# Bias rows of a decoder layer: one broadcast store to DRAM becomes a small store and a copy inside DRAM

## The chip, the cores and the metric

The kernel runs on one core of a Trainium2 chip. The metric is the device time of one execution in microseconds (us), taken as the median of several runs. The profile is one more execution, recorded instruction by instruction. The engines are named as the profile names them: PE is TensorE's matmul, PEld its weight load, DVE is VectorE, ACT is ScalarE, POOL is GpSimd and SP is SyncE, which here only issues transfers. POOL and SP each have a transfer queue of their own (q0 "software" and q1 "hardware" in the profile); both run on the same 16 DMA engines.

## The reference, cut to what matters

One decoder layer for 512 tokens of width 2048. An input projection gives a gated convolution and the queries, keys and values of three groups of eight attention heads. Each group attends with its own dilation (1, 4 and 16 tokens), and to its scores a bias is added that depends on the distance between query and key alone:

```python
steps = qi + BLK - ki
in_window = (steps >= 0) & (steps <= n_steps)
bucket = _t5_bucket(np.clip(steps, 0, None) * dilation)
bias = jnp.take(bias_table, jnp.asarray(bucket), axis=0)
...
scores = scores + bias[:, None]
scores = jnp.where(valid, scores, jnp.finfo(jnp.float32).min)
```

The three groups are mixed by their softmax denominators, an output projection and a LayerNorm follow, then a gated MLP with a width-3 convolution and a second LayerNorm. Everything is float32.

## The kernel before, in words

**The projection.** The 96 column tiles of the input projection are worked off as 48 pairs: twelve for the convolution (u, c, b four times), then 36 for q, k and v. `run_pairs` computes one pair as seven Strassen-like products; each is 24 matmuls in `product` (lines 326 to 328), so a pair has 168. The weights of a pair come as two loads of 1 MB (`load_next`, line 156) into a ring of three `raw` buffers, issued on SP; a load waits until the ring's oldest buffer has been read. `Op.front` and `Op.back` form differences of weights where the product needs them (line 181), round them to `whi` (line 191, ACT) and take the rest as `wlo` (line 194, DVE). There are four `whi` and four `wlo` buffers, so ACT and DVE can be up to four products ahead of PE.

**The outputs of a pair.** About two products after the last one that a half needs, `combine` adds PSUM and a snapshot into a tile `o` of 128 x 1024 (line 572 for q, k, v of group 0, line 581 for the others; the profile names it by these lines). `done1` then stores it: to `yc_d` (line 606) for the convolution, to `qkv_d` (line 611) for q, k and v, both on POOL's queue. The tiles `o` come from a pool of three buffers (`otile1`); a new one waits until the last reader of that buffer is done, which for a store is its landing.

**The bias rows.** After the last convolution pair `bias_setup` runs for the three groups, one every seven products. It takes one of the three `o` buffers as scratch, loads a one-hot matrix (line 555) and a mask (line 556) into it on SP's queue, and five products later `finish` multiplies the bias table with the one-hot matrix (line 560), adds the mask (line 561) and leaves eight rows, one for each head, in partitions 0 to 7: 383 numbers for group 0, 255 for groups 1 and 2. Line 563, on POOL's queue, stores each row 128 times into `seq_d`. Between two calls of `bias_setup` the pairs take `o` buffers from the same pool: the buffer of group 0's rows is next used by the second q, k, v pair, and the scratch of group 2 is the buffer of the first such pair, free when that pair's `qkv_d` store has landed.

**The reader.** `seq_d` is read in the attention, by `toep` in `a_load` (lines 634 to 637): with a step of 383 elements from one copy to the next, each of the 128 partitions reads its row shifted by one, which gives the bias of a block of queries and keys.

The order of the work is that of the program: each engine runs its instructions in the order written, and `later` and `tick` place the deferred parts by a count of products.

Of the kernel before, what the change touches and what calls it, by code (L numbers as in the profile page):

```python
# [12 lines left out]
F32 = mybir.dt.float32  # L13
# [5 lines left out]
P = 128  # L19
# [3 lines left out]
NH = 8  # L23
# [72 lines left out]
def layer_kernel(ctx: ExitStack, tc: tile.TileContext, xT, x, w_in, w_out, w_up, w_down, cw, fw, lnp, lnc, table,  # L96
                 onehot, mask, out):
    nc = tc.nc
# [6 lines left out]
    dram = ctx.enter_context(tc.tile_pool(name="dram", bufs=1, space=bass.MemoryType.DRAM))  # L105
# [15 lines left out]
    def get_bank():  # L121
        i = free_banks.pop(0)
        return i, bank(i)
# [4 lines left out]
    n_d = dram.tile([4, P, D], F32, name="n_d")  # L128
    act_d = dram.tile([P, FT, S], F32, name="act_d")
    seq_d = dram.tile([3, NH, P, 384], F32, name="seq_d")  # L130
    stA_d = dram.tile([NH, S, 2], F32, name="stA_d")
    stB_d = dram.tile([NH, S, 2], F32, name="stB_d")

# [158 lines left out]
    def later(n, fn):  # L292
        pending.append([n, fn])
# [205 lines left out]
    i, b = get_bank()  # L499
# [45 lines left out]
    def otile1():  # L545
        return tp.tile([P, 4, 256], F32, tag="o", name=nm("o"), bufs=3)

    def bias_setup(g=0):
        if g == 0:
            held["tb"] = tp.tile([32, 3 * NH], F32, name="tb")  # L550
            nc.gpsimd.dma_start(held["tb"], table)
        a, b = [0, LA, LA + LB, LTOT][g:g + 2]
        v = otile1().rearrange("p a b -> p (a b)")
        oh, mk = v[:32, 0:b - a], v[:NH, 512:512 + b - a]
        nc.sync.dma_start(oh, onehot[:, a:b])
        nc.sync.dma_start(mk, mask[:, a:b])

        def finish():
            i, ps = get_bank()
            mm(ps[:NH, :b - a], held["tb"][:, g * NH:(g + 1) * NH], oh, start=True, stop=True)  # L560
            nc.vector.tensor_add(mk, ps[:NH, :b - a], mk)
            free_banks.append(i)
            nc.gpsimd.dma_start(seq_d[g, :, :, :b - a], mk[:, None].to_broadcast([NH, P, b - a]))
            if g < 2:
                later(2, lambda: bias_setup(g + 1))

        later(5, finish)
# [505 lines left out]
    for q in range(NQ - 1):  # L1073
        for c in range(4):
# [3 lines left out]
            if c == 1 and q + 2 < NQ:  # L1078
                if q == 0:
                    load_gb(0)  # L1080
                b = (q + 2) % 3
# [118 lines left out]
```

## Time and profile before

| | us |
|---|---|
| median of 3 runs | 2673.99 (2672.46 to 2676.1) |
| the profiled execution's own time | 2674.91 |
| its span, first to last instruction | 2673.0 |
| PE busy in the span | 2624.3 (98%) |
| DVE, ACT, POOL busy | 2015.5, 1159.3, 124.4 |

The mean granted clock of TensorE is 0.992 of full speed. A busy PE is not a PE at full speed: at half the clock its instructions take longer and count as busy all the same, so the number of matmuls in a stretch says more than its busy time. The projection's pairs for q, k and v begin at about 265 us and end at about 1020 us.

### The profile page before, as it was taken

What the parts mean: (1) busy time and instruction counts of PE and PEld (TensorE: products, weight loads), DVE (VectorE), ACT (ScalarE), POOL (GpSimd) and SP (SyncE); (2) the same over time, 40 slices, a digit from 0 to 9 for tenths busy, and PEclk for the clock granted to TensorE, in tenths of its full rate; (3) what the DMA queues carried; (4) which work ended last, traced back from release to release, by engine and by line L of the source; (5) the groups of instructions that cost most, each with busy time, mean ns of one, the idle gap of its engine ahead of it and who ended that gap; (6) DMA issues with size and microseconds to landing.
All of it is one profiled execution on the core that took longest, in us unless ns stands there. A gap on an engine that the chain in (4) does not pass through costs nothing.

```text
span 2673.0 us, 45078 instructions
## 1 busy us (share of the span) xinstructions
PE 2624.3 (98%) x19114; PEld 2497.2 (93%) x19114; DVE 2015.5 (75%) x2293; ACT 1159.3 (43%) x1617; POOL 124.4 (5%) x214
## 2 busy tenths in 40 slices
PE   9999889999999999999999999999999999999998
PEld 8999789999999998888999999999999998888886
DVE  7987557777777777666899888888888875675557
ACT  5444334444444444434655555555555553222220
POOL 0000000000000002221000000000000000000000
PEclk9999989999999999999999999999999999999999
DMA  7433653333333338644543333333333354434331
GB/s 240 166 103 128 111 138 125 134 129 132 135 123 139 134 119 312 221 160 160 182 144 131 117 123 111 123 123 108 126 119 111 127 181 156 149 142 148 120 126 63
DMA packets 70905, 376.69 MB, mean 141 GB/s; under 512 B 10608, under 2 KB 14440, under 8 KB 36016
## 3 DMA queue, kind: packets, MB, share of 16 engines
q1 hardware_dynamic: 51680, 311.47, 34.0%
q0 software_dynamic: 19024, 62.34, 7.3%
q8 instruction: 150, 2.46, 0.4%
q14 instruction: 51, 0.42, 0.1%
HBM read 324.95 MB, written 48.81 MB: 140 GB/s over the span
## 4 chain that ended last, share of the span: by engine, by line
PE 88%; DVE 5%; DMA 4%; ACT 1%; issue 1%; SPq 0%; DVEq 0%; POOL 0%; ACTq 0%
PE bk L326 21%; PE bk L328 21%; PE bk L327 21%; PE bk L423 8%; PE bk L421 8%; PE bk L422 8%; DMA raw<-in_w_in_dram 2%; DMA seq_d<-o 2%; DVE wlo L194 1%; DVE tt L181 1%; PE bk L744 1%; PE bk L690 1%; PE bk L674 0%; ACT whi L191 0%; PE bk L736 0%
## 5 line engine op out<-in xcount | busy, mean ns | idle before, releaser
L191 ACT ACTIVATE whi<-raw 128x1024 fp32r<-128x1024 f32 x394 | 416.0, 1058 | 631.9 <-PE bk L423 219.0
L194 DVE TENSOR_TENSOR wlo<-raw,whi 128x1024 fp32r<-128x1024 f32 x394 | 480.7, 1223 | 216.0 <-ACT whi L191 215.9
L194 DVE TENSOR_TENSOR wlo<-tt,whi 128x1024 fp32r<-128x1024 f32 x360 | 440.5, 1224 | 210.1 <-ACT whi L191 209.5
L191 ACT ACTIVATE whi<-tt 128x1024 fp32r<-128x1024 f32 x360 | 379.6, 1054 | 220.1 <-PE bk L327 122.7
L326 PE MATMUL bk<-S,whi 128*128 128x256 f32 x1440 | 409.2, 284 | 12.4 <-ACT sm L374 11.5
L327 PE MATMUL bk<-S,whi 128*128 128x256 f32 x1440 | 408.4, 284 | 0.0
L328 PE MATMUL bk<-S,wlo 128*128 128x256 f32 x1440 | 408.4, 284 | 0.0
L326 PEld LDWEIGHTS bk<-S,whi 128*128 128x128 f32 x1440 | 277.5, 193 | 13.6 <-ACT sm L374 11.9
L327 PEld LDWEIGHTS bk<-S,whi 128*128 128x128 f32 x1440 | 277.5, 193 | 0.0
L328 PEld LDWEIGHTS bk<-S,wlo 128*128 128x128 f32 x1440 | 277.4, 193 | 0.0
L181 DVE TENSOR_TENSOR tt<-raw,tt 128x1024 f32<-128x1024 f32 x180 | 219.1, 1217 | 36.6 <-DMA raw<-in_w_in_dram 36.6
L326 PE MATMUL bk<-A22h,whi 128*128 128x256 f32 x752 | 212.8, 283 | 0.0
L327 PE MATMUL bk<-A22l,whi 128*128 128x256 f32 x752 | 212.8, 283 | 0.0
L328 PE MATMUL bk<-S3h,wlo 128*128 128x256 f32 x752 | 212.8, 283 | 0.0
L327 PE MATMUL bk<-S3l,whi 128*128 128x256 f32 x752 | 212.8, 283 | 0.0
L326 PE MATMUL bk<-S3h,whi 128*128 128x256 f32 x752 | 212.8, 283 | 0.0
L328 PE MATMUL bk<-A22h,wlo 128*128 128x256 f32 x752 | 212.8, 283 | 0.0
L328 PE MATMUL bk<-S1h,wlo 128*128 128x256 f32 x720 | 205.1, 285 | 6.2 <-DVE wlo L194 6.2
L326 PE MATMUL bk<-A1h,whi 128*128 128x256 f32 x720 | 205.2, 285 | 0.6 <-ACT S L932 0.6
L326 PE MATMUL bk<-S1h,whi 128*128 128x256 f32 x720 | 204.7, 284 | 0.0
L327 PE MATMUL bk<-S1l,whi 128*128 128x256 f32 x720 | 204.7, 284 | 0.0
L328 PE MATMUL bk<-A1h,wlo 128*128 128x256 f32 x720 | 204.4, 284 | 0.0
(225 smaller groups left out, 6435.4 us busy)
## 6 DMA issues: line engine op xcount, KB each, us to landing
raw<-in_w_in_dram SPq DMA_DIRECT2D x97, 1024.0 KB, 4.9
raw<-in_w_up_dram SPq DMA_DIRECT2D x89, 1024.0 KB, 5.3
raw<-in_w_down_dram SPq DMA_DIRECT2D x44, 1024.0 KB, 4.9
qkv_d<-o POOLq DMA_DIRECT2D x36, 512.0 KB, 4.3
raw<-in_w_out_dram SPq DMA_DIRECT2D x16, 1024.0 KB, 6.8
act_d<-z POOLq DMA_DIRECT2D x44, 256.0 KB, 5.2
qk<-qkv_d SPq DMA_DIRECT2D x7, 1536.0 KB, 10.3
ar<-act_d SPq DMA_DIRECT2D x9, 1024.0 KB, 7.0
```

The source lines that it names most:

```text
L181: nc.vector.tensor_sub(self.src, v[0], prev)
L191: nc.scalar.activation(self.hi, self.src, AF.Copy)
L194: nc.vector.tensor_sub(self.lo, self.src, self.hi.bitcast(F32))
L326: mm(ps, op.hi[:, w], xh[:, k], start=first and k == 0, stop=False, skip_group_check=True)
L327: mm(ps, op.hi[:, w], xl[:, k], start=False, stop=False, skip_group_check=True)
L328: mm(ps, op.lo[:, w], xh[:, k], start=False, stop=last and k == 7, skip_group_check=True)
L421: mm(banks[n], yh[:, tt], op.hi[:, w], start=first and i == 0, stop=False)
L422: mm(banks[n], yh[:, tt], op.lo[:, w], start=False, stop=False)
L423: mm(banks[n], yl[:, tt], op.hi[:, w], start=False, stop=last and i == 1)
L690: mm(ps[:, o:o + P], qk[:, 2 + 2 * g, rs], qk[:, 3 + 2 * g, rs], start=True, stop=True)
L744: nc.tensor.transpose(ps[:, i * P:(i + 1) * P], src[:, n, s:s + P], ident)
```

## The change

The eight rows go once into a new DRAM tensor `seq1_d`. A second transfer, from DRAM to DRAM, makes the 128 copies in `seq_d`; its outer loop runs over the 128 copies and the heads lie inside it. Both are on POOL's queue, and the second reads what the first has written. The contents of `seq_d` and its readers are as before.

```diff
     seq_d = dram.tile([3, NH, P, 384], F32, name="seq_d")
+    seq1_d = dram.tile([3, NH, 384], F32, name="seq1_d")
...
             nc.vector.tensor_add(mk, ps[:NH, :b - a], mk)
             free_banks.append(i)
-            nc.gpsimd.dma_start(seq_d[g, :, :, :b - a], mk[:, None].to_broadcast([NH, P, b - a]))
+            nc.gpsimd.dma_start(seq1_d[g, :, :b - a], mk)
+            nc.gpsimd.dma_start(seq_d[g, :, :, :b - a].rearrange("h p n -> p h n"),
+                                seq1_d[g, None, :, :b - a].to_broadcast([P, NH, b - a]))
             if g < 2:
                 later(2, lambda: bias_setup(g + 1))
```

## Rows read from the trace of the kernel before

**Rows 1.** The page: PE's busy time, and the chain's shares by line.
```profile
PE 2624.3 (98%) x19114; PEld 2497.2 (93%) x19114; DVE 2015.5 (75%) x2293; ACT 1159.3 (43%) x1617; POOL 124.4 (5%) x214
...
PE bk L326 21%; PE bk L328 21%; PE bk L327 21%; PE bk L423 8%; PE bk L421 8%; PE bk L422 8%; DMA raw<-in_w_in_dram 2%; DMA seq_d<-o 2%; DVE wlo L194 1%; DVE tt L181 1%; PE bk L744 1%; PE bk L690 1%; PE bk L674 0%; ACT whi L191 0%; PE bk L736 0%
```
**Rows 2.** The chain in order of time, 278 to 380 us: start, length, what.
```profile
278.90 40.53 DMA seq_d<-o
```
**Rows 3.** Stretches: length, busy time and count per engine, PEclk, DMA share, GB/s.
```profile
280.00:400.00 120.00, 96.30 (x731) 94.08 (x730) 63.57 (x64) 36.30 (x47) 5.86 (x8) 0.89 0.60 126
400.00:520.00 120.00, 120.00 (x1002) 120.00 (x1002) 88.43 (x86) 51.00 (x66) 4.29 (x6) 1.00 0.37 130
...
300.00:310.00 10.00, 8.69 (x73) 8.49 (x72) 3.81 (x4) 2.27 (x3) 1.10 (x1) 1.00 0.60 124
```
**Rows 4.** Timeline of DVE, four of its instructions between 262 and 320 us.
```profile
262.22 0.68 DVE L572 TENSOR_TENSOR o<-bk,sm 128x512 f32<-128x512 f32 x1
...
283.30 0.68 DVE L572 TENSOR_TENSOR o<-bk,sm 128x512 f32<-128x512 f32 x1
...
303.98 1.23 DVE L181 TENSOR_TENSOR tt<-raw,tt 128x1024 f32<-128x1024 f32 x1 [9.07 <-DMA raw<-in_w_in_dram]
...
319.46 0.69 DVE L572 TENSOR_TENSOR o<-bk,sn 128x512 f32<-128x512 f32 x1 [11.67 <-DMA seq_d<-o]
```
**Rows 5.** Waits, 255 to 420 us: who <- whom: us, times, longest.
```profile
PE bk L326 <- ACT sm L374: 10.6, 1, 10.6
...
PE bk L560 <- DMA o<-in_onehot_dram: 6.9, 1, 6.9
...
PE bk L328 <- DVE wlo L194: 6.2, 2, 4.9
```
**Rows 6.** DMA issues, 279 to 308 us: times, KB each, median us to landing.
```profile
raw<-in_w_in_dram SPq DMA_DIRECT2D x2, 1024.0 KB, 21.3
...
qkv_d<-o POOLq DMA_DIRECT2D x1, 512.0 KB, 36.7
```
**Rows 7.** DMA issues of the whole span (columns of Rows 6).
```profile
raw<-in_w_in_dram SPq DMA_DIRECT2D x97, 1024.0 KB, 4.9
...
qkv_d<-o POOLq DMA_DIRECT2D x36, 512.0 KB, 4.3
...
gb<-in_lnp_dram SPq DMA_DIRECT2D x4, 1024.0 KB, 9.1
...
seq_d<-o POOLq DMA_DIRECT2D x1, 1532.0 KB, 40.5
...
stA_d<-st POOLq DMA_DIRECT2D x8, 4.0 KB, 6.3
...
tb<-in_table_dram POOLq DMA_DIRECT2D x1, 3.0 KB, 2.8
```
**Rows 8.** Timeline of SP's queue: two weight loads, 281.54 and 11 us later.
```profile
281.54 11.20 SPq L156 DMA_DIRECT2D raw<-in_w_in_dram  x2
```
**Rows 9.** The waits of SP's queue, 255 to 425 us.
```profile
SPq L555 <- DMA qkv_d<-o: 28.2, 1, 28.2
```
**Rows 10.** Timeline of POOL: start, length, instruction, [idle before <-releaser].
```profile
278.90 1.10 POOL L563 DMA_DIRECT2D seq_d<-o  x1 [13.40 <-DVE o L561]
284.28 0.74 POOL L611 DMA_DIRECT2D qkv_d<-o  x1 [4.28 <-DVE o L572]
...
398.94 0.72 POOL L611 DMA_DIRECT2D qkv_d<-o  x1 [17.16 <-DVE o L581]
419.09 0.71 POOL L611 DMA_DIRECT2D qkv_d<-o  x1 [19.44 <-DVE o L581]
```
**Rows 11.** A stretch with one `seq_d` store alone (columns of Rows 3).
```profile
290.00:293.00 3.00, 3.00 (x27) 3.00 (x27) 1.86 (x2) 1.52 (x3) 0.00 (x0) 1.00 0.48 49
```
**Rows 12.** DMA queue, 308 to 318 us: packets, MB, share of 16 engines.
```profile
q0 software_dynamic: 132, 0.58, 91.8%
```
**Rows 13.** Users of `seq_d`: ns min/median/max, first and last start in us.
```profile
L634 POOL DMA_DIRECT2D ba<-seq_d x1: 553/553/553, 1008.5 to 1008.5; - x1
```

## The prediction, as it was put on record before the result was known

> **What bounds the kernel now.** I read the page first. PE is busy for 98% of the span and its matmul lines make up nearly all of the chain, so only what stops PE, or slows it, can move the time; but one transfer stands in that chain too, the store of the bias rows, with 2% [rows 1]. The chain in order of time shows where: group 0's store, issued at 278.90 us, is 40.53 us of it in one piece [rows 2]. So I took the stretch around it and compared it with the next one of the same length: 731 matmuls in 280 to 400 us against 1002 in 400 to 520 us, with a mean granted clock of 0.89 against 1.00 [rows 3]. PE idles there, and for part of the time after it idled it runs at the lower of its two levels. The question is how much of that is the three stores' doing, and whether the copies that replace them do the same again.
>
> The waits of the stretch name three ways in which a store of 40 us reaches PE. First, the scratch: `o` stays taken until the store lands, and DVE's combine waits 11.67 us for it [rows 4]; PE then stands 10.6 us behind the snapshot [rows 5]. Second, the weights: two loads of 1 MB took 21.3 us to land [rows 6] where the median of 97 is 4.9 [rows 7]; DVE waited 9.07 us for the one issued at 281.54 [rows 4, 8], and later PE stood 6.2 us for weights of this kind [rows 5]. Third, the queue: the first pair's `qkv_d` store, issued behind the bias store, took 36.7 us to land [rows 6]; SP waited 28.2 us for it before it could load group 2's one-hot matrix [rows 9], and PE 6.9 us for that matrix [rows 5].
>
> **What the change can give back.** The q, k, v stores are a clock of the pairs. From 398.94 to 419.09 one pair takes 20.15 us [rows 10]. From 284.28 to 419.09 there are five pairs (the stores at 323, 353 and 381 us are not shown): 134.81 us less 5 x 20.15 leaves 34.06. Not all of it is a stall: the bias matmuls themselves cost PE something, and group 0's price, before any bias store was in flight, is the distance from the combine at 262.22 to that at 283.30, 21.08 less 20.15 = 0.93 us [rows 4]. Groups 1 and 2 keep that: 1.86. So 32.2 us are stall. By matmuls it is 120 x (1002 - 731) / 1002 = 32.5 us, less 1.86 = 30.6 [rows 3]. I take the middle, 31.4 us, and both as ends. Idle time and the lower clock behind it are both in these numbers.
>
> **What it adds, step by step.**
>
> The small store, 12 KB from eight partitions: no row has this shape. The nearest are a 3 KB load on the same queue, 2.8 us to landing, and 4 KB of statistics stored in pieces of 8 bytes, 6.3 us [rows 7]. It is a store, but with rows of 1.5 KB; I take 4 us. It frees the scratch at about 283 instead of 319.4. The second pair's combine came for it at 319.46 - 11.67 = 307.8, and without the weights' 9 us before that would come at about 299. The first of the three ways is gone, for any price between the two ends.
>
> The wait on POOL: the copy reads what the store wrote, so POOL stands until that lands, 278.90 + 4 = 282.9. The copy's issue takes the 1.10 us of the present one [rows 10], up to 284.0. Queued behind is only the `qkv_d` store of 284.28 [rows 10], so this costs nothing; at 6.3 us it would be issued 2 us late, and nobody needs it for another 8.
>
> The copy itself, 1532 KB for group 0. No row moves DRAM to DRAM. From below: a 1 MB load lands in 4.9 us, so 1.5 MB hardly in less than 7.3. From above: the present store of the same rows, 40.5 us [rows 7]. Which end is nearer depends on why the store is slow. Alone, it keeps 0.48 of the DMA engines busy and moves 49 GB/s [rows 11]; when two overlap, the engines are 91.8% busy and the same queue moves 0.58 MB in 10 us, 58 GB/s [rows 12]. Twice the engines gave hardly more rate, so the limit is shared: either the eight source partitions or the rows written. The q, k, v stores write DRAM at well over that, 512 KB in 4.3 us or 119 GB/s with all their fixed cost [rows 7], but out of 128 partitions and in longer rows; the few partitions are the larger difference, and I take the source as the cause. The copy's source is instead one stretch of 12 KB in DRAM read 128 times. That has a near row: `gb` reads one DRAM row 128 times, 1 MB in 9.1 us to landing, four of them, issued in pairs by line 1059 [rows 7]. I take 9.1 x 1532 / 1024 = 13.6 us, and 9.1 for groups 1 and 2 (1020 KB).
>
> What waits for the copies. The readers of `seq_d` come at 1008.5 [rows 13], 700 us later: nothing. The first pair's `qkv_d` store lies behind the copy on the queue: 282.9 + 13.6, and about 4 for itself, is 300.5. SP waits for it from about 292.7 (320.95 less 28.2), and behind that wait on SP is the next weight load, due at 281.54 + 20.15 = 301.7: nothing lost. The one-hot matrix is then there by about 306, and its matmul is due two pairs after group 0's, which the store of 278.90 followed, so not before 317.
>
> The weight load of 281.54 runs beside the copy. If it got no engine at all until the copy had landed, it would land at 282.9 + 13.6 + 4.9 = 301.4 against the 294.9 at which DVE asked for it (303.98 less 9.07): 6.5 us late. That is covered: DVE's 9.07 us of waiting cost PE only 10 - 8.69 = 1.3 us in 300 to 310 [rows 3], because ACT and DVE work ahead of PE by some 7.8 us. Groups 1 and 2 meet the same pattern 20 and 40 us later with shorter copies. So a copy costs nothing up to about 13.6 - 6.5 + 7.8 = 14.9 us, and I cost all three at nothing; the cover is the 7.8 us of finished weights.
>
> **The sum** against the profiled execution: 2674.91 - 31.4 = 2643.5 us. That execution is 0.9 above the median of the runs shown, 2673.99; from there it is 2642.6. I say 2643. About 0.2%, 5.3 us, is what a measurement of this kernel can tell from no change.
>
> [...] One bias store alone holds only 0.48 of the engines, and two 0.92 [rows 11, 12]: a weight load had half of the engines free. [...]
>
> For how long weights wait beside such a transfer, the row is 21.3 us to landing instead of 4.9 [rows 6, 7]. [...]
>
> **The rivals.** Let D be the time of group 0's copy, and two thirds of it for the others, and let weights get nothing while a copy runs. PE then idles D - 14.9 for group 0, and 0.67 D - 14.9 for each of the others, where these are above nothing. In the present stretch PE's idle time, 120 - 96.3 = 23.7 us [rows 3], went with a loss of 31.4, so each us idle costs 1.3.
>
> *All engines are held for a middling time.* The copy takes about 22 us, because it reads and writes the same memory and its rows are 1.5 KB: 22 - 14.9 = 7.1 us idle, times 1.3, is 9 us given back: 2652. For it: no row shows such a copy. Against it: `gb` moves more than three times as fast. Chance 0.10.
>
> *The written rows are the limit, and it becomes slower.* If the 128 x 8 rows of 1532 bytes were what held the store to 49 GB/s, the copy would be no faster, and it would hold all engines. Then 40.5 - 14.9 = 25.6 and 2 x 12.2 are 50.0 us idle, 65 with the clock, against 31.4 now: 2708. It decides from D = 29 on, where 2.34 D - 44.7 reaches 23.7. For it: the two causes leave the same rate. Against it: the first pair's store of 512 KB and other DRAM writes share these engines and land in a few us elsewhere. Chance 0.08.
>
> *It does not do what it says.* The copy, D between 27 and 31, is as long as the stall that it replaces, or the scratch stays taken because the small store lands late in a busy queue: within 5 us of 2674. Chance 0.06.
>
> **How the numbers follow.** The forecast has 0.76, and its own spread is 2639 to 2647 (30.6 to 32.2, the runs' own 2 us, a few us for one stall that I miss). The first rival has 0.10 at 2652. The range 2639 to 2657 takes in both and leaves out the two others, 0.14, and some of the tails. Faster by over 0.2%: 0.76 + 0.10 = 0.86; within: 0.06; slower: 0.08.
>
> **What would show it.** In the profile after: no wait of DVE for `seq_d` or `seq1_d`, no wait of SP for `qkv_d` at line 555, about 990 matmuls in 280 to 400 us with a clock of 1.00, five pairs in some 102.7 us from the first `qkv_d` store, and copies that land in 7 to 14 us. A copy over 20 us, or weight loads that still land in over 15, would show the first rival; copies of 30 us and more the second. The forecast is wrong if PE still idles in this stretch for more than a few us.

## The result, and the profile after

The changed kernel takes 2643.47 us (median of four runs, 2643.22 to 2643.77), the kernel before 2674.87 beside it. The ratio is 0.9884, with a 95% interval of 0.9867 to 0.9901: 31.4 us, 1.2%, faster.

The page of the changed kernel, its first part and its chain by line:

```profile
PE 2616.5 (99%) x19114; PEld 2490.2 (94%) x19114; DVE 2016.7 (76%) x2293; ACT 1159.4 (44%) x1617; POOL 125.8 (5%) x217
...
PE bk L327 22%; PE bk L328 22%; PE bk L329 22%; PE bk L424 8%; PE bk L422 8%; PE bk L423 8%; DVE wlo L195 1%; DVE tt L182 1%; PE bk L747 1%; DMA raw<-in_w_in_dram 1%; PE bk L693 0%; ACT whi L192 0%; PE bk L677 0%; DMA ycr<-yc_d 0%; PE bk L739 0%
```

Lines are shifted by one to three against before. `seq_d` is gone from the chain [rows 1]. PE was busy longer before (2624.3 us) with the same 19114 matmuls: some of them had run at the lower clock (0.89 granted in 280 to 400 us [rows 3]). What that does to a busy PE two stretches of the kernel before show: 11 matmuls from 324 to 326 us at a clock of 0.50, 19 from 328 to 330 us at 1.00, and PE counts as busy for all of both.

The stretches that answer to [rows 3] (length, busy time and count per engine, PEclk, DMA share, GB/s):

```profile
280.00:400.00 120.00, 120.00 (x994) 118.87 (x993) 87.19 (x85) 49.99 (x65) 8.16 (x11) 1.00 0.49 163
400.00:520.00 120.00, 120.00 (x1002) 120.00 (x1001) 86.96 (x85) 51.05 (x66) 4.30 (x6) 1.00 0.38 132
300.00:310.00 10.00, 10.00 (x85) 10.00 (x85) 7.45 (x8) 3.72 (x5) 1.64 (x2) 1.00 0.68 201
```

994 matmuls stand where 731 stood, at full clock, and PE does not idle. POOL's timeline, the new pair of transfers and the stores that mark the pairs (start, length, instruction, [idle before <-releaser]):

```profile
278.72 0.52 POOL L564 DMA_DIRECT2D seq_d<-o  x1 [13.38 <-DVE o L562]
280.69 0.94 POOL L565 DMA_DIRECT2D seq_d<-seq_d  x1 [1.45 <-DMA seq_d<-o]
284.10 0.74 POOL L614 DMA_DIRECT2D qkv_d<-o  x1 [2.48 <-DVE o L575]
...
387.23 0.72 POOL L614 DMA_DIRECT2D qkv_d<-o  x1 [19.45 <-DVE o L584]
```

From 284.10 to 387.23 there are five pairs, 103.13 us; before they took 134.81 [rows 10]. That difference, 31.7 us, is the whole change: from the sixth such store to the end it is 2673.0 - 419.1 = 2253.9 us before and 2641.7 - 387.2 = 2254.5 after. POOL waits 1.45 us for the small store to land, then issues the copy, and is idle again before the next `qkv_d` store is ready: nothing waits for it.

The transfers issued from 279 to 308 us (times, KB each, median us to landing), which answer to [rows 6]:

```profile
raw<-in_w_in_dram SPq DMA_DIRECT2D x3, 1024.0 KB, 5.0
seq_d<-seq_d POOLq DMA_DIRECT2D x1, 1532.0 KB, 11.1
qkv_d<-o POOLq DMA_DIRECT2D x2, 512.0 KB, 8.2
seq_d<-seq_d POOLq DMA_DIRECT2D x1, 1020.0 KB, 9.5
o<-in_onehot_dram SPq DMA_DIRECT2D x1, 31.9 KB, 4.3
seq_d<-o POOLq DMA_DIRECT2D x1, 12.0 KB, 1.7
```

The copy lands in 11.1 us instead of 40.5, the weights in 5.0 (median of three) instead of 21.3 (of two), the `qkv_d` stores in 8.2 (of two) instead of 36.7. Of SP's waits for a transfer this one is left (255 to 425 us: who <- whom: us, times, longest), where 28.2 stood [rows 9]:

```profile
SPq L556 <- DMA qkv_d<-o: 0.4, 1, 0.4
```

### The profile page after: what moved, and what is told of

It is laid out like the page before. It is cut to its first block, busy times and chain, and to the rows that moved or that the text cites. A ratio compares the mean times of both kernels' runs of the same rounds, so it can differ in the third digit from the quotient of the medians.

```text
span 2641.7 us, 45080 instructions
## 1 busy us (share of the span) xinstructions
PE 2616.5 (99%) x19114; PEld 2490.2 (94%) x19114; DVE 2016.7 (76%) x2293; ACT 1159.4 (44%) x1617; POOL 125.8 (5%) x217
## 4 chain that ended last, share of the span: by engine, by line
PE 91%; DVE 5%; DMA 1%; ACT 1%; issue 1%; SPq 0%; POOL 0%; DVEq 0%; ACTq 0%
PE bk L327 22%; PE bk L328 22%; PE bk L329 22%; PE bk L424 8%; PE bk L422 8%; PE bk L423 8%; DVE wlo L195 1%; DVE tt L182 1%; PE bk L747 1%; DMA raw<-in_w_in_dram 1%; PE bk L693 0%; ACT whi L192 0%; PE bk L677 0%; DMA ycr<-yc_d 0%; PE bk L739 0%
## 5 line engine op out<-in xcount | busy, mean ns | idle before, releaser
L328 PE MATMUL bk<-A1l,whi 128*128 128x256 f32 x720 | 204.4, 284 | 0.0
```

Of the source, the lines that this page charges most:

```text
L328: mm(ps, op.hi[:, w], xl[:, k], start=False, stop=False, skip_group_check=True)
```

## The experiments

The times of the experiments are medians of four to ten runs, with the kernel before timed on the same chip (2673.8 to 2674.0 us; 2674.87 for the changed kernel). "Store" is the time to landing of group 0's bias store or copy, "weights" that of the first weight load issued beside it, "matmuls" the count in 280 to 400 us; these three are from one profiled execution each. The ratios are against the kernel before; no interval was taken between two edits.

| run | edit | us | ratio, 95% interval | store | weights | matmuls |
|---|---|---|---|---|---|---|
| before | | 2674 | | 40.5 | 22.3 | 731 |
| after | the change | 2643.5 | 0.9867 to 0.9901 | 11.1 | 8.6 | 994 |
| e4_fullrows | whole rows written | 2673.3 | 0.9984 to 1.0003 | 39.6 | 22.3 | 741 |
| e6_from128 | store from 128 partitions | 2643.6 | 0.9873 to 0.9902 | 7.1 | 9.8 | 993 |
| e9_spread4 | from 8, four apart | 2642.7 | 0.9868 to 0.9899 | 13.4 | 9.8 | 995 |
| e10_spread16 | from 8, sixteen apart | 2643.1 | 0.9869 to 0.9904 | 23.0 | 14.5 | 989 |
| e5_heads_outer | copy, heads outside | 2647.0 | 0.9881 to 0.9914 | 13.5 | 5.3 | 995 |
| e1_scratch | own scratch | 2670.6 | 0.9978 to 0.9997 | 41.8 | 23.0 | 768 |
| e2_actq | store on ACT's queue | 2667.6 | 0.9966 to 0.9985 | not recorded | 21.1 | 791 |
| e3_both | both | 2661.6 | 0.9936 to 0.9966 | not recorded | 21.4 | 839 |
| e7_copy2 | two copies | 2648.0 | 0.9889 to 0.9919 | 19.2 (both) | 9.6 | 995 |
| e8_copy4 | four copies | 2644.0 | 0.9880 to 0.9909 | 32.7 (all) | 9.5 | 931 |
| e11_held | four copies, scratch held | 2662.1 | 0.9939 to 0.9970 | 32.4 (all) | 9.5 | 846 |

### Why the store was slow

**The rows written (e4_fullrows).** Edit, on the kernel before (the mask gets one column more, and the sum leaves that column as loaded):

```diff
-            nc.gpsimd.dma_start(seq_d[g, :, :, :b - a], mk[:, None].to_broadcast([NH, P, b - a]))
+            nc.gpsimd.dma_start(seq_d[g, :, :, :b - a + 1], mk[:, None].to_broadcast([NH, P, b - a + 1]))
```

> The kernel before, storing rows of 384 and 256 numbers (1536 and 1024 bytes) instead of 383 and 255, so that each row written is whole and follows the last without a gap; the extra number is a mask value that no reader uses. Theory, the eight source partitions set the store's rate: still about 40 and 24 to 34 us to land, about 49 GB/s alone, 2675 us within 4. Rival, the written rows with their gaps set it: under 20 us to land and under 2655.

Nothing changed: 39.6 us to landing, and 2673.3 us. The gaps between the rows do not set the rate; the rows themselves are tested next.

**The source partitions (e6_from128, e9_spread4, e10_spread16).** The three are one store out of SBUF, as before. Their table has each head's column repeated, so that the matmul leaves the row in several partitions; what is stored differs. For e9_spread4 (the mask row is loaded into all partitions):

```diff
-            held["tb"] = tp.tile([32, 3 * NH], F32, name="tb")
-            nc.gpsimd.dma_start(held["tb"], table)
+            tb = tp.tile([32, 3 * NH], F32, name="tb")
+            nc.gpsimd.dma_start(tb, table)
+            held["tb"] = tp.tile([32, 3 * 32], F32, name="tbr")
+            nc.vector.tensor_copy(held["tb"].rearrange("p (h c) -> p h c", c=4),
+                                  tb[:, :, None].to_broadcast([32, 3 * NH, 4]))
...
-            nc.gpsimd.dma_start(seq_d[g, :, :, :b - a], mk[:, None].to_broadcast([NH, P, b - a]))
+            nc.gpsimd.dma_start(seq_d[g, :, :, :b - a], mk[::4, None].to_broadcast([NH, P, b - a]))
```

e10_spread16 has 16 in place of 4, and e6_from128 stores all 128 partitions eight times each:

```diff
+            nc.gpsimd.dma_start(seq_d[g].rearrange("h (c r) n -> (h c) r n", r=8)[:, :, :b - a],
+                                mk[:, None].to_broadcast([P, 8, b - a]))
```

> One broadcast store from SBUF as in the kernel before, on POOL's queue, but out of 128 partitions: the bias table's columns are repeated 16 times, so that the matmul leaves each head's row in 16 partitions, and each partition is stored eight times. The rows written are the same; there is no copy in DRAM and no wait on POOL. Theory, the eight source partitions set the rate: lands in 5 to 12 us, 2643 us within 4. Rival, the written rows set it: about 40 us and 2670 or over.

The question to the two spread stores is whether the number of the source partitions held the store or their place; that the place would count was my estimate, and no run had shown it then.

> The store of the kernel before, in the same order and with the same outer loop of eight heads, but the eight source rows lie in partitions 0, 4, 8 ... 28 instead of 0 to 7 (the bias table's columns are repeated four times, and every fourth row is stored). [...] Rival, each partition gives only so much whichever it is: still about 40 us, 2674. [...]

> The same with the eight source rows in partitions 0, 16, 32 ... 112, repeated sixteen times. [...] Rival, any spreading is as good, or the wider the better: 8 to 12 us. [...]

All three are as fast as the changed kernel within 1 us, with no copy in DRAM. The row to compare is POOL's DMA queue in the same three us, 281 to 284 (packets, MB, share of 16 engines). The kernel before:

```profile
q0 software_dynamic: 316, 0.16, 56.3%
```

e9_spread4:

```profile
q0 software_dynamic: 470, 0.62, 57.4%
```

The rows written, their order and, within two per cent, the busy share of the engines are the same, and four times as many bytes go out. In the store only the eight source partitions differ. So neither the written rows nor the number of engines held the store; reading from neighbouring partitions did. The landing times are 40.5 us for 0 to 7, 23.0 for steps of sixteen, 13.4 for steps of four and 7.1 for all 128. "Farther apart" would have put the step of sixteen ahead of the step of four, so it is not the distance alone that counts; what else does, no run shows. I had taken the eight partitions as the cause; eight of them elsewhere gave 13.4 us, so it is not their number alone but where they lie.

**The outer loop (e5_heads_outer).** Edit, on the changed kernel:

```diff
-            nc.gpsimd.dma_start(seq_d[g, :, :, :b - a].rearrange("h p n -> p h n"),
-                                seq1_d[g, None, :, :b - a].to_broadcast([P, NH, b - a]))
+            nc.gpsimd.dma_start(seq_d[g, :, :, :b - a],
+                                seq1_d[g, :, None, :b - a].to_broadcast([NH, P, b - a]))
```

> The changed kernel, with the heads instead of the copies as the outer loop of the DRAM to DRAM copy: the same rows are read and written, in another order. Theory, the source partitions made the store slow: the copy stays fast, landing in 8 to 16 us with half of the engines or more, and the time is that of the changed kernel, 2643 us within 4. Rival, an outer loop of eight (half of the engines) made it slow: 30 us and more to land, and 2655 or over.

The copy lands in 13.5 us, and alone it keeps half of the engines busy (a stretch of e5_heads_outer, columns of [rows 3]):

```profile
290.00:293.00 3.00, 3.00 (x28) 3.00 (x27) 1.34 (x2) 1.33 (x2) 0.00 (x0) 1.00 0.52 202
```

Group 0's weight load lands in 5.3 us beside it instead of 8.6, but group 2's in 8.5 instead of 9.6, so what the free engines are worth to a load is not settled. PE gains nothing from them: 995 matmuls, full clock. The 3.5 us above the changed kernel lie elsewhere. The profiled execution is 4.7 us longer; 1.3 of them have passed when the first `qkv_d` store is issued, and 3.6 lie between the last `qkv_d` store and the last `v` load of the attention, 157.8 us against 154.2. At the start of that stage the load of `yc_d` takes 12.96 us instead of 10.93. The pairs between the first and the last `qkv_d` store take as long as in the changed kernel, 706.0 us.

### How a slow store reached PE

**Own scratch (e1_scratch).** Edit, on the kernel before:

```diff
         oh, mk = v[:32, 0:b - a], v[:NH, 512:512 + b - a]
+        if g < 2:
+            mk = tp.tile([P, 384], F32, tag="bs", name=nm("bs"), bufs=2)[:NH, :b - a]
```

> The kernel before, but the sums of groups 0 and 1 lie in buffers of their own, so that the slow store no longer holds a buffer that the pairs need (group 2 stays as it was). Theory, three ways that stand in a row: the 11.7 us wait of DVE for the scratch goes, but the first pair's qkv_d store still lands at about 321 us behind the bias store, SP still stands for it, and the weights come late instead: about 2668 us, between 2661 and 2675. Rival, the held scratch is the whole stall: 2643 to 2650 us. The bias stores themselves still take 24 to 41 us to land.

2670.6 us: 3.4 of 31 us come back. The waits of e1_scratch, 255 to 420 us (who <- whom: us, times, longest):

```profile
DVE tt L181 <- DMA raw<-in_w_in_dram: 44.2, 3, 22.5
...
PE bk L328 <- DVE wlo L194: 21.6, 3, 14.8
```

DVE's wait for the scratch is gone, and so is SP's for the `qkv_d` store, because group 2's one-hot matrix went into a buffer that group 1's matmul had freed. In their place DVE waits 44.2 us for weights where it had waited 36.6, and PE 21.6 for what DVE makes of them where it had waited 6.2 [rows 5]. The kernel before, in the same view:

```profile
DVE tt L181 <- DMA raw<-in_w_in_dram: 36.6, 3, 15.5
```

So e1_scratch came out as the third way alone, and that alone costs 2670.6 - 2643.5 = 27 us. It is the third way in a stronger form: SP, no longer held up, issues two loads at 310 to 317 us, beside two bias stores, and they take 31.7 and 29.5 us; the kernel before issued them at 322 us and later, and the first took 23.3.

**Another queue (e2_actq, e3_both).** Edit, alone and on top of e1_scratch:

```diff
-            nc.gpsimd.dma_start(seq_d[g, :, :, :b - a], mk[:, None].to_broadcast([NH, P, b - a]))
+            nc.scalar.dma_start(seq_d[g, :, :, :b - a], mk[:, None].to_broadcast([NH, P, b - a]))
```

> The kernel before, with the bias stores issued on ACT's queue instead of POOL's; the scratch is held as before. Theory: the first pair's qkv_d store no longer lies behind the bias store and lands in under 10 us, SP does not stand for it at the one-hot load, and the 6.9 us wait of PE for the one-hot matrix goes; the wait of DVE for the scratch (about 11 us) and late weights stay: about 2661 us, between 2655 and 2670. Rival, the queue does not matter because the weights are what is late: over 2670.

> Both edits at once: bias stores on ACT's queue, the sums of groups 0 and 1 in buffers of their own. Only the third way is left, weights that share engines with a slow store. Theory: weight loads beside a bias store still take 12 to 22 us to land, 4 to 9 us too late for DVE, which the finished weights mostly cover: 2645 to 2652 us. Rival, the slow weights are a stall of their own: over 2655.

e2_actq gives back 6.4 us, in the range, but not quite as expected: the `qkv_d` store lands in 19.8 us instead of 36.7, not in under 10, and SP still stands 11.3 us for it. The bias store was still busy beside it, on ACT's queue, with 44.4% of the engines (283 to 285 us); that this is the reason is likely, and no run shows it. e3_both missed, 2661.6 instead of 2645 to 2652. Its waits show the rival's picture, slow weights as a stall of their own:

```profile
DVE tt L181 <- DMA raw<-in_w_in_dram: 35.2, 3, 16.5
...
PE bk L328 <- DVE wlo L194: 13.8, 3, 9.6
```

It is no clean test of the third way, since SP stood 12.2 us for a `qkv_d` store and 8.6 us for a bias store before it issued weights.

**The first two ways without the third (e11_held).** Edit, on e8_copy4 below: behind the four copies a store of the scratch, which therefore stays taken until they are through.

```diff
+            nc.gpsimd.dma_start(last_d[g, :, :b - a], mk)
```

> The kernel with four copies, and behind them on POOL's queue one more small store out of the scratch, so that the scratch stays taken until the copies are through, some 35 us, as with the store of the kernel before; there is no slow packet for the weights to stand behind. The first two ways without the third. Theory now, each way alone is enough for a stall: DVE waits for the scratch by 10 to 16 us in group 0 and again later, 2658 to 2675 us. Rival, only the slow weights made the stall and the scratch costs little alone: under 2652.

In e11_held a packet of POOL's queue kept an engine busy for 0.19 us (44.4% of 16 engines for 13 us, 478 packets, from 279 to 292 us), in the kernel before for 0.67 (48.9% of 16 for 5 us, 58 packets, from 288 to 293 us). That a weight load stands behind such a packet no run shows.

2662.1 us, 18.6 above the changed kernel. The waits of e11_held name the scratch (DVE's combine is L581 here) and hardly the weights:

```profile
DVE o L581 <- DMA last_d<-o: 27.5, 2, 14.7
...
PE bk L329 <- ACT sm L377: 14.3, 2, 8.1
...
DVE tt L184 <- DMA raw<-in_w_in_dram: 0.2, 1, 0.2
```

Late weights alone cost 27 us, held scratch with the blocked queue 19, and all together 31. The ways overlap: while PE stands for one, the others run out. That is why undoing one or two of them gave little. The blocked queue nearly alone is e8_copy4 below: 0.5 us in the median of four runs, 7 in one of them.

### What a long copy costs

**More copies (e7_copy2, e8_copy4).** Edit, on the changed kernel, with j up to 1 or 3:

```diff
+            for j in range(3):
+                nc.gpsimd.dma_start(more_d[j, g, :, :, :b - a].rearrange("h p n -> p h n"),
+                                    seq1_d[g, None, :, :b - a].to_broadcast([P, NH, b - a]))
```

> The changed kernel with a second copy, to another DRAM tensor, behind each copy. Theory, a copy costs nothing up to about 14.9 us: the last of group 0's copies lands 15 to 18 us after the first was issued, the qkv_d store behind it by about 300 us, and the time stays within 4 us of 2643. Rival, each us of copy costs something: 2650 or over.

> The changed kernel with three more copies behind each copy, to other DRAM tensors. Theory: group 0's copies together last about 26 us, the others about 19; beyond 14.9 us each us of copy idles PE and costs 1.3: 11 x 1.3 for group 0, 4 x 1.3 for each of the others, 2667 us, between 2655 and 2680; SP stands for the qkv_d store at the one-hot load again. Rival, weights and copies take turns and the cover holds: 2643 to 2650.

e7_copy2 lies 4.5 us above the changed kernel, just outside "within 4". Its stretch has no stall, 995 matmuls at full clock, and as in e5_heads_outer the attention is longer, 158.0 us. e8_copy4 contradicts the expectation: copies that last 32.7 us together take 2644.0 us in the median, as the rival said, and not 2667. Its four runs are 2643.3, 2643.8, 2644.2 and 2650.7, and the last is the profiled one. There the first weight load beside the copies lands early (issues from 279 to 292 us: times, KB each, median us to landing):

```profile
more_d<-seq_d POOLq DMA_DIRECT2D x3, 1532.0 KB, 27.6
seq_d<-seq_d POOLq DMA_DIRECT2D x1, 1532.0 KB, 14.0
raw<-in_w_in_dram SPq DMA_DIRECT2D x1, 1024.0 KB, 9.5
qkv_d<-o POOLq DMA_DIRECT2D x1, 512.0 KB, 30.4
```

The `qkv_d` store takes 30.4 us, nearly as long as beside the slow store, and SP stands 22.0 us for it. The weight load takes 9.5 us, not 22.3, and the second one, issued 11 us later, 13.4 instead of 20.2. PE works through all of this at full clock until 320 us. What the profiled execution loses comes after it: because SP stood, its next weight load goes out at 316.85 us instead of 302.27 in the changed kernel, and takes 13.0 us beside group 1's copies. The waits of e8_copy4, 255 to 420 us:

```profile
DVE tt L183 <- DMA raw<-in_w_in_dram: 21.8, 3, 13.9
...
PE bk L330 <- DVE wlo L196: 6.1, 1, 6.1
```

So in this execution the long copies reached PE by the queue, the second way. Why the three other runs escape stays open, since none of them has a trace.

In the view of the issues from 279 to 292 us, e10_spread16:

```profile
seq_d<-o POOLq DMA_DIRECT2D x1, 1532.0 KB, 23.0
raw<-in_w_in_dram SPq DMA_DIRECT2D x1, 1024.0 KB, 14.5
qkv_d<-o POOLq DMA_DIRECT2D x1, 512.0 KB, 19.7
```

Its second load takes 10.8 us. The two first loads thus take 22.3 and 20.2 us beside the slow store of 40.5, 14.5 and 10.8 beside a store of 23.0, and 9.5 and 13.4 beside 32.7 us of copies that, with the loads, keep 0.97 of the engines busy from 283 to 288 us. How long the other transfer lasts does not set this; its pace is the likelier cause, but the last two cases lie too close to show that. How the slow store delays a load can be seen in part. From 288 to 293 us of the kernel before, with one load out since 281.54, the queues have this one line:

```profile
q0 software_dynamic: 58, 0.26, 48.9%
```

That is POOL's queue. SP's moved no packet, though the engines were idle for half of the time.

## Why the prediction was right, and where a step was not

The forecast was 2643 us, and 2643.47 was measured.

**The size of the stall** was right: 31.4 us forecast, from 32.2 by the stores and 30.6 by the matmuls; 31.7 us went from the five pairs. What stayed, 103.13 - 5 x 20.15 = 2.4 us, is the bias matmuls' 1.86 and half a us.

**The scratch and the queue** were right. The small store was taken at 4 us and took 1.7, so the wait on POOL was 1.45 instead of 4. SP's wait for the `qkv_d` store came out as 0.4 us; the store landed at 293.0, not at 300.5.

**The copy** was taken at 13.6 and 9.1 us and took 11.1 and 9.5. The reason given for it, the source partitions, held: e4_fullrows excludes the gaps between the rows, and e6_from128 and e9_spread4 write the same rows fast from other partitions. That their place counts, 40.5 us from 0 to 7 and 13.4 from steps of four, the prediction had not said; "few" was not the point. One argument against the first rival was misread: `gb` moves 1 MB in 9.1 us, which is 1.6 times the pace of a copy of 22 us, not "more than three times"; it is the present store that it beats threefold.

**All engines held** was the first rival. That a copy holds them all was an assumption, and no row showed it. The copy with a loop of eight kept 0.52 of them busy (e5_heads_outer, 290 to 293 us), like the store with its 0.48 [rows 11]; the copies with a loop of 128 kept 1.00 busy in e8_copy4 from 300 to 312 us, for part of that with a weight load beside them. It costs nothing while the copies are short, 11.1 us here. That a copy takes 22 us, because it reads and writes the same memory, no run shows either.

**The step that failed** is a premise, that "weights get nothing while a copy runs", and with it the limit worked out from it, "So a copy costs nothing up to about 13.6 - 6.5 + 7.8 = 14.9 us". In e8_copy4 the first load landed 9.5 us after its issue, at 291.3 us, while the copies ran until 313.8, and until 320 us PE stood for nothing. Loads and copies moved side by side: from 283 to 290 us of the changed kernel POOL's queue kept 55.2% of the engines busy and SP's 43.2%. The first loads beside copies with a loop of 128 landed in 8.6 to 9.6 us, about twice the 4.9 of the median load [rows 7], and the second in e8_copy4 in 13.4; what sets these times no run shows. So the first rival was priced too high; a copy as slow as the second rival's no run made. The 21.3 us of the row belong to the slow store and did not carry over to a copy. The forecast did not hang on this, because the copy stayed under even the wrong limit.

**The cover** of 7.8 us itself held well. In e8_copy4 DVE waited 13.85 us for weights and PE then 6.1. In e1_scratch the waits of 9.70 and 22.53 us cost PE 1.94 and 14.8. That is 7.7 to 7.8 us less each time. In e10_spread16, where no wait for weights was longer than 6.9 us, they cost PE nothing. What long copies did cost, in the one run of e8_copy4, came by the queue: the `qkv_d` store behind them landed at 315 us, and SP's next weight load was due at about 302.

**The order of the three ways** was not settled by the profile. I listed the weights last, with 6.2 us of PE's waiting, and expected own scratch and another queue together to leave only a few us. They left 18, and the weights alone cost 27. A waits view shows what ended each wait, not what would have ended it next.

Open: why the attention takes 3.6 to 3.9 us more in the profiled executions of e5_heads_outer and e7_copy2. The load of `yc_d` is longer in both, 12.96 and 13.24 us against 10.93, and no run tells why. What follows from it can be read: from 990 to 996 us PE is idle 2.1 and 2.4 us instead of 0.3, and behind that some of its matmuls run at the lower level, 0.43 us each instead of 0.23. From 992 to 1002 us the mean granted clock is 0.83 instead of 1.00, which is worth another 1.7 us by estimate (0.17 of 10 us).

## What to carry to other kernels

A broadcast store out of eight neighbouring partitions was slow at 1.5 MB (40.5 us) and at 1 MB (24.3 us and more). Spread the rows (four apart, 2642.7 us, is as good here as a copy in DRAM, 2643.5, and needs no wait), or store them once and copy. Look at what a slow transfer holds, a buffer, a queue and the engines that other loads need, and undo it at the source: taking away one of these waits gave back 3.4 or 6.4 of 31 us here and let the next one show. Long copies at a high rate delayed the first load beside them less than the slow store did, 9.5 us to landing (e8_copy4) against 22.3, but the `qkv_d` store behind them on their queue took 30.4; look there for what a long transfer costs.

## What the runs showed of the hardware

- The eight rows left SBUF four times as fast from partitions 0, 4 ... 28 as from 0 to 7, 0.62 against 0.16 MB in three us, with the same share of the DMA engines busy (57.4 and 56.3%). With steps of sixteen the store landed in 23.0 us, between 13.4 and 40.5.
- A weight load of 1 MB took 22.3 us to land beside the store from neighbouring partitions and 14.5 beside the one with steps of sixteen. Beside the faster stores and copies of group 0 it took 5.3 to 9.8 us, and the next one, beside 33 us of copies, 13.4; the median of all 97 loads before is 4.9 [rows 7].
- Beside the slow store a load of 1 MB that had been issued at 281.54 moved no packet from 288 to 293 us, while the store kept the DMA engines busy for 48.9% of the time.
- A copy of one 12 KB stretch of DRAM into 128 places, 1.5 MB, landed in 11.1 us beside a weight load; that all of it was read from one stretch did not make it as slow as the store, 40.5.
